# Four edits in one decoder layer: output weights split earlier, two transposition turns inside products, one FFN weight prepared ahead, the last roots on ScalarE and VectorE

## The chip, the cores and the metric

One core of one Trainium2 chip runs the program. The metric is device microseconds for one execution. PE is the matrix engine (TensorE), PEld its weight loads, DVE VectorE, ACT ScalarE, POOL GpSimd, SP the engine whose queue issues most of the transfers.

## What is computed

One layer of a decoder for a prompt group (16 meta tokens and 512 tokens) and a sample group (8 sequences of 8 new tokens with 2048 cached ones). D_MODEL is 1024, D_FF 2816. In the words of the reference:

```python
xn = rmsnorm(x, p['ln_mix_pre'])
h = xn @ p['w_in']                        # q, k, v, DeltaNet inputs and two gates
o_a = differential attention of q, k, v   # with its own rmsnorm
o_b = gated DeltaNet of the rest          # with its own rmsnorm
mix = jax.nn.sigmoid(gate_a) * (o_a @ p['w_branch_a']) + jax.nn.sigmoid(gate_b) * (o_b @ p['w_branch_b'])
x = x + rmsnorm(mix @ p['w_out'], p['ln_mix_post'])
xn = rmsnorm(x, p['ln_ffn_pre'])
up, gate = jnp.split(xn @ p['w_ffn_in'], 2, axis=-1)
gate, new_ffn_conv = causal_dwconv(gate, ffn_conv_buf, p['ffn_conv_w'], p['ffn_conv_b'])
x = x + rmsnorm((jax.nn.gelu(gate) * up) @ p['w_down'], p['ln_ffn_post'])
```

The new keys, values, states and convolution tails are outputs too. All arrays are float32.

## The kernel before

**Products.** Every float32 product is three matmuls of halves: high by high, high by low, low by high. `split` (L311 to L314) makes the halves: ScalarE copies the array rounded into `hi` (L313), VectorE subtracts that from the array into `lo` (L314). Weights come through `load_w` (L306 to L309) in blocks of 256 KB into a ring of three raw slots (`wraw`); a slot is free once cast and subtract have read it. The blocks are issued on SP's queue, each in its turn. `whi` has 2 slots and `wlo` 4. PSUM is handed out by tags (d, t, g, s); two d banks alternate.

**Order.** The program is written stage by stage; a scheduler of the framework turns it into one fixed list for each engine, and an engine that waits holds up what is behind it in its list. The last part of `main` and what follows:

- the gates, then `branch_a`, the attention branch: 8 tiles m of 128 output channels, each as two parts of 256 and 322 tokens (`branch`), a part being 12 matmuls. Behind each part a VectorE multiply-add (L1532) takes the PSUM bank into the gate's array, which frees the bank.
- `mix`: the same 8 tiles for the DeltaNet branch; then the sum of both branches (L1564) and its split for the output projection. Behind tiles 2 to 5 `load_wout` loads and splits two blocks each of the first half of w_out (`owhi`, `owlo` of `wo0`): 8 loads, 8 casts, 8 subtracts.
- `out_proj`: `product(i, g)` multiplies token tile i (0 is the sample group) by half g of w_out, 24 matmuls of 512 columns; `finish(i)` scales, adds the residual, and scales again for the FFN into `y`; `turn(i)` transposes `y` by 8 matrix-engine transposes in two groups of four, each group in a PSUM bank, and casts and splits the banks (`fhi`, `flo`). `product(4,0)` stands behind `turn(1)`. At its end come the first gate product `g0`, the first up product `u0` and `turn(4)`.
- `ffn_in`: the FFN tiles. The up weight of tile 1 is split at its start, in `plain_w` (`hw`, `lw`), and is first used right behind `turn(4)`.
- `ffn_out`: the down projection for five token tiles. The end of each is `known` and `finish`: sums of squares to a root, then the scaling of `yn` and its transfer out. The root is a power on GpSimd (`pow` with -1/2, L2175).

**Rooms.** `gt` is a ring of 18 arrays that the mixed activations use until the output projection is over; `flot2` is one of the arrays that the FFN's first stage uses later.

## Time and profile before

| what | us |
|---|---|
| median of 3 runs | 1143.41 (1142.62 to 1145.4) |
| profiled execution | 1143.95 |
| its span | 1142.2 |
| PE busy in the span | 1113.5 |
| DVE, ACT, POOL busy | 727.1, 524.7, 224.8 |

The granted matrix clock was 0.998 of full speed. The span runs from the first to the last instruction of the profiled execution; the 1.75 us between span and time lie around it. Times within the span count from its start. A timeline row reads: start, length, engine, line, operation, written array <- read arrays, size, count; in brackets how long the engine stood idle before it and who released it. One row may hold several instructions (x2), and lengths of neighbours may overlap by a tenth of a microsecond, since a next one starts before the last has written all. A matmul row's length is modelled, so the step from one start to the next is what it costs.

### The profile page before, as it was taken

The page shows a single profiled execution, that of the slowest core. Times are in us where ns is not written, and L with a number is a line of the kernel's source. Part 1 is how long each engine was busy: PE and PEld are TensorE (multiplying, and loading weights), DVE is VectorE, ACT ScalarE, POOL GpSimd, SP SyncE. Part 2 cuts the span into 40 slices and gives each one's busy share as a digit, 9 for nine tenths or more (in the row PEclk, how much of TensorE's full clock was granted, in tenths as well). Part 3 has the DMA queues.
Part 4 walks back from the last instruction along what each step waited for, and adds up shares of the span by engine and source line. Part 5 has one row for each costly group of instructions (what it writes and reads, how often), then busy time and mean ns, then how long its engine had stood idle before and what let it go on. Part 6 is the DMA issues. An engine that isn't in the chain of part 4 may idle for free.

```text
span 1142.2 us, 22715 instructions
## 1 busy us (share of the span) xinstructions
PE 1113.5 (97%) x8263; PEld 976.5 (85%) x8263; DVE 727.1 (64%) x1876; ACT 524.7 (46%) x1257; POOL 224.8 (20%) x349
## 2 busy tenths in 40 slices
PE   8999999999999999999999999999999999999997
PEld 6987897787787787789999977899999999988885
DVE  5466656695585386474343765499999999842314
ACT  5244454464465365352342444365555555732211
POOL 3122221120120020010000003334445454200000
PEclk9999999999999999999999999999999999999999
DMA  6376426837746856822232364223333232333203
GB/s 191 82 247 183 121 71 207 275 103 257 243 150 216 289 168 215 261 72 76 56 88 72 114 183 149 87 87 94 101 93 105 87 103 75 115 109 102 98 33 120
DMA packets 167610, 156.97 MB, mean 137 GB/s; under 512 B 12540, under 2 KB 123715, under 8 KB 167498
## 3 DMA queue, kind: packets, MB, share of 16 engines
q1 hardware_dynamic: 162833, 147.14, 41.7%
q0 software_dynamic: 3264, 5.16, 1.5%
q10 hardware_dynamic: 1400, 3.22, 0.9%
q8 instruction: 65, 1.06, 0.4%
q14 instruction: 48, 0.39, 0.1%
HBM read 145.60 MB, written 9.88 MB: 136 GB/s over the span
## 4 chain that ended last, share of the span: by engine, by line
PE 75%; issue 13%; DVE 5%; ACT 3%; POOL 3%; DMA 1%; POOLq 0%; DVEq 0%; SPq 0%; ACTq 0%
PE ps_d L271 27%; PE ps_t L271 19%; PE ps_g L271 15%; PE ps_s L271 6%; PE ps_t L419 6%; ACT KT L1419 1%; PE ps_m L271 1%; DVE cy L670 1%; POOL grr L383 1%; POOL gf L383 0%; DMA page<-in_cache_v 0%; POOL hss L383 0%; DVE row L990 0%; DVE row L991 0%; DVE xc L992 0%
## 5 line engine op out<-in xcount | busy, mean ns | idle before, releaser
L314 DVE TENSOR_TENSOR wlo<-wraw,whi 128x512 fp32r<-128x512 f32 x190 | 143.1, 770 | 117.8 <-ACT whi L313 117.1
L271 PE MATMUL ps_d<-xhi,whi 128*128 128x256 f32 (+2 forms) x704 | 217.2, 309 | 0.4 <-ACT xhi L313 0.3
L271 PE MATMUL ps_d<-xhi,wlo 128*128 128x256 f32 (+2 forms) x704 | 212.8, 302 | 0.5 <-POOL wlo L314 0.5
L271 PE MATMUL ps_d<-xlo,whi 128*128 128x256 f32 (+2 forms) x704 | 212.2, 302 | 0.3 <-DVE xlo L314 0.3
L313 ACT CAST whi<-wraw 128x512 fp32r<-128x512 f32 x194 | 116.3, 621 | 174.9 <-PE ps_d L271 81.1
L271 PEld LDWEIGHTS ps_d<-xhi,whi 128*128 128x128 f32 x704 | 132.9, 189 | 6.2 <-issue 3.8
L271 PEld LDWEIGHTS ps_d<-xlo,whi 128*128 128x128 f32 x704 | 133.3, 189 | 3.2 <-issue 2.4
L271 PEld LDWEIGHTS ps_d<-xhi,wlo 128*128 128x128 f32 x704 | 133.1, 189 | 2.4 <-issue 1.0
L314 DVE TENSOR_TENSOR lw<-sw,hw 128x512 fp32r<-128x512 f32 x76 | 69.2, 911 | 5.9 <-ACT hw L313 5.9
L1419 ACT COPY KT<-ps_t 128x512 f32<-128x512 f32 x106 | 57.2, 603 | 31.2 <-PE ps_t L419 30.7
L419 PE MATMUL ps_t<-consts,page 128*128 128x128 f32 x512 | 67.8, 279 | 0.3
L271 PE MATMUL ps_t<-fhit,hw 128*128 128x290 f32 x228 | 68.0, 298 | 0.0
L271 PE MATMUL ps_t<-flot,hw 128*128 128x290 f32 x228 | 67.7, 297 | 0.0
L271 PE MATMUL ps_t<-fhit,lw 128*128 128x290 f32 x228 | 67.6, 297 | 0.0
L419 PEld LDWEIGHTS ps_t<-consts,page 128*128 128x128 f32 x512 | 55.5, 140 | 13.6 <-issue 6.7
L313 ACT CAST hw<-sw 128x512 fp32r<-128x512 f32 x76 | 47.0, 618 | 32.9 <-PE ps_g L271 15.7
L271 PEld LDWEIGHTS ps_t<-flot,hw 128*128 128x128 f32 x228 | 43.2, 190 | 0.0
L271 PEld LDWEIGHTS ps_t<-fhit,lw 128*128 128x128 f32 x228 | 43.1, 189 | 0.0
L271 PEld LDWEIGHTS ps_t<-fhit,hw 128*128 128x128 f32 x228 | 43.0, 189 | 0.0
L271 PE MATMUL ps_s<-page,pT 128*32 128x256 f32 x512 | 35.3, 385 | 2.0 <-DMA page<-in_cache_v 1.8
L1912 DVE SCALAR_TENSOR_TENSOR fy<-fpre,fw,fy 128x592 f32<-128x592 f32 x44 | 36.5, 829 | 1.0 <-ACT fy L1910 0.4
L271 PE MATMUL ps_s<-KT,qb 128*32 128x256 f32 x512 | 35.7, 385 | 0.6
(688 smaller groups left out, 2847.9 us busy)
## 6 DMA issues: line engine op xcount, KB each, us to landing
page<-in_cache_k SPq DMA_DIRECT2D x128, 256.0 KB, 4.1
page<-in_cache_v SPq DMA_DIRECT2D x128, 256.0 KB, 4.5
wraw<-in_w_in SPq DMA_DIRECT2D x88, 256.0 KB, 3.0
wraw<-in_w_ffn_in SPq DMA_DIRECT2D x50, 256.0 KB, 3.0
wraw<-in_w_down SPq DMA_DIRECT2D x44, 256.0 KB, 2.6
raw<-in_w_ffn_in SPq DMA_DIRECT2D x38, 256.0 KB, 2.8
wraw<-in_w_out SPq DMA_DIRECT2D x16, 256.0 KB, 2.7
x<-in_x_prompt SPq DMA_DIRECT2D x4, 512.0 KB, 6.8
```

Of the source, the lines that this page charges most:

```text
L271: return self.nc.tensor.matmul(out, lhsT, rhs, **kw).ins
L313: self.nc.scalar.copy(hi, raw)
L314: (eng or self.nc.vector).tensor_tensor(out=lo, in0=raw, in1=hi.bitcast(F32), op=ALU.subtract)
L383: nc.gpsimd.tensor_tensor(out=dst, in0=dst, in1=self.mhalf[:rows, :n], op=ALU.pow)
L419: self.nc.tensor.transpose(out, in_, self.ident[:k, :k])
L670: nc.vector.scalar_tensor_tensor(out=y, in0=pre[:, j : j + n], scalar=self.cw[:, ch, 24 + j : 25 + j], in1=y, op0=ALU.mult, op1=ALU.add)
L1419: copy(kt[:, :, 128 * j : 128 * j + 128], tp)
L1912: nc.vector.scalar_tensor_tensor(out=y, in0=pre[:, j : j + 592], scalar=fw[:, m, 16 + j : 17 + j], in1=y, op0=ALU.mult, op1=ALU.add)
```

## The change

- **Output weights.** The arrays of w_out's first half are allotted before the attention branch. A new function `wout_ahead` issues the blocks, two after each tile m of `branch_a`, up to four times; what is left of the four would follow in `mix` from tile 2 on.
- **Turns.** `turn(0)` is issued inside `product(2,1)` and `turn(1)` inside `product(3,0)`, after k = 3 (`MID`), that is after 12 of 24 matmuls.
- **FFN weight.** The up weight of tile 1 is loaded and split at the end of `out_proj`, its high half into `flot2`, its low half into two arrays of the `gt` ring; `turn(4)` now stands amid the product that uses it.
- **Last roots.** `finish` of `ffn_out` takes Sqrt on ScalarE, then one Newton step with two reciprocals on VectorE. Sqrt needs its function table; a first Sqrt on zeros at the start of `ffn_out` brings the load there.

```diff
                         yield from self.mix_parts(self.pool(s2, "mix"))
+                        self.wo0 += self.wout_tiles(self.pool(swo, "wo0", side="right"), 0)
...
             for half in HALF_Q:
                 self.branch(m, 1, x, half)
                 yield 0.0
+            self.wout_ahead()
...
+    def wout_ahead(self):
+        if self.wo0 and self.wo_next < 4:
+            self.load_wout(self.wo0, 0, self.wo_next)
+            self.wo_next += 1
...
-            if 2 <= m < 6:
-                self.load_wout(wo0, 0, m - 2)
+            if m >= 2:
+                self.wout_ahead()
...
                 end = self.mm(p[:n], ml, whi[:, k], start=False, stop=k == 7)
+                if between and k == MID:
+                    turn(between[0], end, between[1])
...
-        product(2, 1)
+        product(2, 1, (0, "t"))
         finish(2)
-        turn(0, ends[2, 1])
-        product(3, 0)
-        turn(1, ends[3, 0])
+        product(3, 0, (1, "t"))
         product(4, 0)
...
+        hi, los = self.t(self.ftpool, [128, 8, 128], "flot2", F32R), []
+        for k, raw in zip((0, 4), self.raw_w(a["w_ffn_in"][0], 128)):
+            lo = self.t(self.gtpool, [128, 4, 128], "gt", F32R, bufs=18)
+            self.split(hi[:, k : k + 4], lo, raw)
+            los += [lo[:, j] for j in range(4)]
...
-        sts[1]["wu"] = plain_w(0, 1)
...
+        roots = [self.t(pool, [128, 5], f"yroot{j}") for j in range(3)]
+        nc.scalar.activation(roots[1], ss[:, :, 0], AF.Sqrt)
...
-            nc.gpsimd.tensor_tensor(out=r[:n], in0=r[:n], in1=self.mhalf[:n, :1], op=ALU.pow)
+            nc.scalar.activation(w, v, AF.Sqrt)
+            nc.vector.reciprocal(u, w)
+            nc.vector.scalar_tensor_tensor(out=v, in0=v, scalar=u, in1=w, op0=ALU.mult, op1=ALU.add)
+            nc.vector.reciprocal(r[:n], v)
```

How this moves instructions, at three places. Lines of the code after are larger by 2 (L314 becomes L316, L1532 becomes L1534, L271 becomes L273, L419 becomes L421).

**VectorE in the attention branch.** Before, each tile has its weight's subtract (`wlo`) and two multiply-adds into the gate's array:

```order
L314 TENSOR_TENSOR wlo_8659<-wraw_8656,whi_8658 128x512 [waits DMAHW3_49,Activation_49]
L1532 SCALAR_TENSOR_TENSOR gt_7253<-gt_7253,ps_d_8621 128x256 [waits PE_49]
L1532 SCALAR_TENSOR_TENSOR gt_7253<-gt_7253,ps_d_8641 128x322 [waits PE_49]
L314 TENSOR_TENSOR wlo_8693<-wraw_8690,whi_8692 128x512 [waits DMAHW4_49,Activation_49]
L1532 SCALAR_TENSOR_TENSOR gt_7489<-gt_7489,ps_d_8655 128x256 [waits PE_49]
```

After, from the subtract of tile 1's weight on (`wlo_8672`; `wlo_8714` is tile 2, `wlo_8756` tile 3; `gt_7253` is tile 0's array, `gt_7489` tile 1's, `gt_7617` tile 2's):

```order
L316 TENSOR_TENSOR wlo_8672<-wraw_8669,whi_8671 128x512 [waits DMAHW5_49,Activation_49]
L1534 SCALAR_TENSOR_TENSOR gt_7253<-gt_7253,ps_d_8626 128x256 [waits PE_49]
L316 TENSOR_TENSOR owlo_1604_8455<-wraw_8744,owhi_1603_8454 128x4x128 [waits DMAHW1_49,Activation_49]
L1534 SCALAR_TENSOR_TENSOR gt_7253<-gt_7253,ps_d_8646 128x322 [waits PE_49]
L316 TENSOR_TENSOR wlo_8714<-wraw_8711,whi_8713 128x512 [waits DMAHW0_49,Activation_49]
L316 TENSOR_TENSOR owlo_1604_8455<-wraw_8748,owhi_1603_8454 128x4x128 [waits DMAHW2_49,Activation_49]
L1534 SCALAR_TENSOR_TENSOR gt_7489<-gt_7489,ps_d_8668 128x256 [waits PE_49]
L1534 SCALAR_TENSOR_TENSOR gt_7489<-gt_7489,ps_d_8688 128x322 [waits PE_49]
L316 TENSOR_TENSOR wlo_8756<-wraw_8753,whi_8755 128x512 [waits DMAHW3_49,Activation_49]
L316 TENSOR_TENSOR owlo_1604_8455<-wraw_8786,owhi_1603_8454 128x4x128 [waits DMAHW4_49,Activation_49]
L1534 SCALAR_TENSOR_TENSOR gt_7617<-gt_7617,ps_d_8710 128x256 [waits PE_49]
```

The subtract of w_out's fifth block (`wraw_8744`) now stands between the two multiply-adds of tile 0, those of the sixth (`wraw_8748`) and seventh (`wraw_8786`) ahead of the first multiply-add of tiles 1 and 2. The eighth stands between tile 2's two. The same loads on SP's queue, from tile 1's weight to tile 3's:

```order
L311 DMA wraw_8669<-in_w_branch_a 128x4x128 [waits DMAHW3_49,DVE_49]
L311 DMA wraw_8702<-in_w_out 128x4x128 [waits DMAHW4_49,DVE_49]
L311 DMA wraw_8706<-in_w_out 128x4x128 [waits DMAHW2_49,DVE_49]
L311 DMA wraw_8711<-in_w_branch_a 128x4x128 [waits DMAHW6_49,DVE_49]
L311 DMA wraw_8744<-in_w_out 128x4x128 [waits DMAHW7_49,DVE_49]
L311 DMA wraw_8748<-in_w_out 128x4x128 [waits DMAHW5_49,DVE_49]
L311 DMA wraw_8753<-in_w_branch_a 128x4x128 [waits DMAHW1_49,DVE_49]
```

Two blocks of w_out stand between the weights of neighbouring tiles; before, the attention weights followed each other without a gap.

**PE around turn 1.** Before, the end of `product(3,0)` (`ps_s_9554`), the two groups of `turn(1)` (`y_9360` is tile 1's `y`), and the start of `product(4,0)`:

```order
L271 MATMUL ps_s_9554<-owhi_1668_8896,gt_9239 128x512
L419 MATMUL ps_t_9583<-consts_66,y_9360 128x128 [waits DVE_49]
L419 MATMUL ps_t_9583<-consts_66,y_9360 128x128 x3
L419 MATMUL ps_t_9588<-consts_66,y_9360 128x128 [waits DVE_49,PE_49]
L419 MATMUL ps_t_9588<-consts_66,y_9360 128x128 x3
L271 MATMUL ps_t_9597<-owhi_1668_8896,gt_8933 128x512 [waits DVE_49,PE_49]
```

After, the same turn with its neighbours, both of `product(3,0)`:

```order
L273 MATMUL ps_s_9554<-owhi_1603_8454,gt_9083 128x512
L421 MATMUL ps_t_9567<-consts_66,y_9360 128x128 [waits DVE_49]
L421 MATMUL ps_t_9567<-consts_66,y_9360 128x128 x3
L421 MATMUL ps_t_9572<-consts_66,y_9360 128x128 [waits DVE_49,PE_49]
L421 MATMUL ps_t_9572<-consts_66,y_9360 128x128 x3
L273 MATMUL ps_s_9554<-owhi_1603_8454,gt_9121 128x512
```

Twelve matmuls of `product(3,0)` now stand between turn 1 and `product(4,0)`, which still takes a t bank; turn 0 stands likewise amid `product(2,1)`.

**PE around turn 4.** Before, the end of the second gate product (`ps_g_9932`), turn 4 (`y_9622`) and the start of the second up product (`ps_s_9959`):

```order
L419 MATMUL ps_t_9874<-consts_66,y_9622 128x128 [waits DVE_49,PE_49]
L419 MATMUL ps_t_9874<-consts_66,y_9622 128x128 x3
L271 MATMUL ps_g_9932<-flo_1739_9255,fhit_1827_9840 128x290
L271 MATMUL ps_g_9932<-fhi_1738_9254,flot_1828_9841 128x290
L419 MATMUL ps_t_9879<-consts_66,y_9622 128x128 [waits DVE_49,Activation_49]
L419 MATMUL ps_t_9879<-consts_66,y_9622 128x128 x3
L271 MATMUL ps_s_9959<-fhi_1734_9250,hw_9916 128x290 [waits Activation_49]
L271 MATMUL ps_s_9959<-flo_1735_9251,hw_9916 128x290
L271 MATMUL ps_s_9959<-fhi_1734_9250,lw_9917 128x290 [waits DVE_49]
```

After, ten products of the second up product (`ps_s_9958`) stand ahead of turn 4:

```order
L273 MATMUL ps_g_9931<-fhi_1738_9254,flot_1828_9841 128x290
L273 MATMUL ps_s_9958<-fhi_1734_9250,flot_1831_9850 128x290
L273 MATMUL ps_s_9958<-flo_1735_9251,flot_1831_9850 128x290
L273 MATMUL ps_s_9958<-fhi_1734_9250,gt_9855 128x290
...
L421 MATMUL ps_t_9885<-consts_66,y_9622 128x128 [waits DVE_49,PE_49]
L421 MATMUL ps_t_9885<-consts_66,y_9622 128x128 x3
L421 MATMUL ps_t_9890<-consts_66,y_9622 128x128 [waits PE_49,Activation_49]
L421 MATMUL ps_t_9890<-consts_66,y_9622 128x128 x3
L273 MATMUL ps_s_9958<-flo_1735_9251,flot_1831_9850 128x290
```

The product's waits on ScalarE and VectorE are gone from its row in the order, and turn 4 stands later in it.

More of the change, by code (lines that the diff above doesn't have):

```diff
@@ L142 @@
 PLAIN = 3
+MID = 3
 KT = 16
@@ L248, in run @@
                     self.banks = "ggsttdd"
-                    swo = ExitStack()
-                    wo0 = self.wout_tiles(self.pool(swo, "wo0", side="right"), 0)
-                    self.mix(wo0)
+                    self.mix()
             sf = ctx.enter_context(ExitStack())
@@ L1593, in out_proj, with product @@
         ys, sums, ends = {}, {}, {}
-        def product(i, g):
+        def product(i, g, between=None):
             c0, n = self.TILES[i]
@@ L1633, in finish, with turn @@
             self.scaled(xs[:n], x[:n], r[:n], lnf[:n], CUT_O)
-        def turn(i, end):
+        def turn(i, end, tag="t"):
             n, xs, ps = self.TILES[i][1], ys.pop(i), []
@@ L1959, in plain_w @@
         def plain_w(c0, m):
-            if m == 1 and c0:
-                return w1
-            if m != 1:
-                return self.weight(w, c0 + 128 * m)
-            his, los = [], []
-            for raw in self.raw_w(w, c0 + 128 * m):
-                hi, lo = (self.t(w7, [128, 4, 128], tag, F32R, bufs=n) for tag, n in (("hw", 6), ("lw", 6)))
-                self.split(hi, lo, raw)
-                his += [hi[:, k] for k in range(4)]
-                los += [lo[:, k] for k in range(4)]
-            return his, los
+            return w1[0 if c0 else 1] if m == 1 else self.weight(w, c0 + 128 * m)
         def copy_g(st, half, ps):
```

17 lines of the change are left out of this document (10 added, 7 removed).

## The prediction

> **What bounds the kernel now.** I read the page first, then busy time by stage, then what PE waited for, then the rows of the four places that the change touches.
>
> ```profile
> span 1142.2 us, 22715 instructions
> PE 1113.5 (97%) x8263; PEld 976.5 (85%) x8263; DVE 727.1 (64%) x1876; ACT 524.7 (46%) x1257; POOL 224.8 (20%) x349
> ```
>
> PE has matrix work in 97% of the span. Whatever shortens the time here either takes work from PE or takes a wait from it; the change takes no product away, so only PE's 28.7 us without work are to be had, and only those at the places it touches. By stage (columns: span, busy PE, PEld, DVE, ACT, POOL, clock, DMA share, GB/s):
>
> ```profile
> 615.18:640.84 25.66, 25.66 (x195) 25.66 (x194) 12.34 (x23) 5.30 (x9) 0.00 (x0) 1.00 0.27 79
> 640.84:671.03 30.19, 27.74 (x200) 26.47 (x199) 25.45 (x45) 15.05 (x29) 0.00 (x0) 1.00 0.47 135
> ...
> 745.40:800.00 54.60, 54.60 (x406) 54.58 (x407) 53.14 (x88) 30.67 (x62) 19.63 (x24) 1.00 0.32 94
> ```
>
> The rows are the attention branch, the mix stage (DeltaNet branch) and the first FFN tiles. PE is full in the first and the last, 2.45 us short in the second. In the last VectorE has 1.5 us to spare in 54.6: a gain made ahead of it must survive it. The waits (engine and line waited for: total, times, longest):
>
> ```profile
> PE ps_d L271 <- ACT whi L313: 1.6, 1, 1.6
> ...
> PE ps_t L419 <- DVE flo L314: 1.2, 1, 1.2
> PE ps_s L271 <- DVE lw L314: 1.0, 1, 1.0
> PE ps_t L271 <- DVE flo L314: 0.7, 1, 0.7
> PE ps_t L271 <- ACT owhi L313: 0.6, 1, 0.6
> ...
> PE ps_s L271 <- ACT hw L313: 0.5, 1, 0.5
> ```
>
> The first and fifth are in the mix stage, the second and fourth behind turn 1, the third and sixth before the second FFN up product.
>
> **1. Output weights split in the attention branch.** What leaves the mix stage: in the attention branch one tile of 8 takes 3.205 us (25.66 / 8). The mix stage has 8 tiles of the same products and took 30.19 us; six output-projection products stood in it (1.4 us at 0.23 each, the step from 712.46 to 712.69 in part 2). 30.19 - 25.64 - 1.4 = **3.15 us** are lost there: 8 loads, casts and subtracts of w_out share the raw ring of three and VectorE (25.45 of 30.19 us busy). Without the 8 subtracts, 0.6 us each in a row, VectorE has about 20.6 us of work for 25.6, and the DeltaNet loads follow each other as the attention loads did before. I count the whole 3.15 as gained.
>
> What the attention branch gets: the same 8 loads, casts and subtracts, and each now stands in VectorE's order ahead of an operation that PE waits for. The order shows the subtract of the fifth w_out half-row block in front of the multiply-add (L1532 before, L1534 after) of tile 0's second part, and this multiply-add frees the PSUM bank for the second part of tile 1.
>
> ```profile
> 615.89 0.69 DVE L314 TENSOR_TENSOR wlo<-wraw,whi 128x512 fp32r<-128x512 f32 x1 [5.66 <-ACT whi L313]
> ...
> 618.59 0.49 DVE L1532 SCALAR_TENSOR_TENSOR gt<-gt,ps_d 128x322 f32<-128x322 f32 x1 [1.37 <-PE ps_d L271]
> ...
> 619.80 0.31 PE L271 MATMUL ps_d<-kt,whi 128*128 128x322 f32 x1
> ...
> 639.05 3.58 SPq L309 DMA_DIRECT2D wraw<-in_w_out  x2
> ...
> 641.96 0.62 ACT L313 CAST owhi<-wraw 128x512 fp32r<-128x512 f32 x1 [0.25 <-DMA wraw<-in_w_out]
> ```
>
> Of the ring's three slots the third load back must be subtracted before the next is issued. SP's order after is tile 2's weights, then w_out blocks 5 and 6; tile 2 reuses the slot of tile 1, free when the wlo of 615.89 ends at 616.58. Issues follow at 0.4 us: 616.6, 617.0, 617.4. From issue to cast took 2.9 us (639.05 to 641.96). So block 5 is cast at 619.9 to 620.5, subtracted (0.69) to 621.15, and the multiply-add (0.49) ends at 621.65; PE wanted the bank at 619.80: **1.85 us of stall** in place of a full PE. Behind the waiting subtract stand on VectorE tile 2's wlo (to 622.2), block 6 and tile 1's multiply-add. Tile 3's load goes out at 622.3, block 7 at 622.7, cast behind tile 3's at 625.75 to 626.35, subtracted to 627.0; the multiply-add behind it (0.42) ends at 627.4, and PE, 1.85 late, wants that bank at 626.65: **0.75**. Tile 4, issued at 626.5, is split by 630.7 and wanted at 630.55: **0.15**. Then VectorE is even with PE. Loss 2.75, net **-0.4 us**. The bounds: no stall (-3.15), if the loads land before their subtracts are due; and for every us that landing is later, each of the three stalls grows by one.
>
> ```profile
> wraw<-in_w_out SPq DMA_DIRECT2D x16, 256.0 KB, 2.7
> ...
> page<-in_cache_v SPq DMA_DIRECT2D x128, 256.0 KB, 4.5
> ```
>
> With 2.7 us, the median of these loads, the loss is 2.75 - 3 x 0.2 = 2.15; with 4.5 us, that of the cache pages under heavy traffic, it is 7.5, net +4.4. The branch moved 79 GB/s and gets some 80 more, so I stay near 2.9. The Trainium skill (DMA: Bandwidth & Descriptors, the section on where the fixed time goes) gives a load about 2.0 us of fixed time, nearly all completion, and bytes at 436 GB/s. Its 256 KB would take 2.6 us, 0.1 under the 2.7 of the row: an estimate by the page is a loss near 1.85 and a sum of -5.5, where I keep the rows' -4.6.
>
> **2. Turns amid products.** A turn is 8 transposes, then casts and subtracts out of two PSUM banks.
>
> ```profile
> 702.96 0.66 PE L419 MATMUL ps_t<-consts,y 66*128 66x66 f32 x8
> ...
> 709.08 0.60 PE L419 MATMUL ps_t<-consts,y 128*128 128x128 f32 x4
> 710.83 0.63 PE L419 MATMUL ps_t<-consts,y 128*128 128x128 f32 x4 [1.16 <-DVE flo L314]
> 712.15 0.47 PE L271 MATMUL ps_t<-owhi,gt 128*128 128x512 f32 x1 [0.69 <-DVE flo L314]
> 712.46 0.39 PE L271 MATMUL ps_t<-owlo,gt 128*128 128x512 f32 x1
> 712.69 0.62 PE L271 MATMUL ps_t<-owhi,gt 128*128 128x512 f32 x2
> ...
> 742.05 0.60 PE L419 MATMUL ps_t<-consts,y 128*128 128x128 f32 x4
> 742.40 0.38 PE L271 MATMUL ps_g<-flo,fhit 128*128 128x290 f32 x1
> ...
> 704.54 0.75 DVE L403 SCALAR_TENSOR_TENSOR y<-xr,r,lnf 128x512 f32<-128x512 f32 x1 [0.67 <-POOL r L383]
> ```
>
> Four transposes take 0.35 us when nothing waits (742.05 to 742.40), so turn 1 and its successor need 0.8 with the restart; they took 712.15 - 709.08 = 3.07. **Gain up to 2.25.** Turn 1 waits for the banks of turn 0, whose subtracts came 3 to 5 us after its transposes, and product (4,0) waits for one of turn 1's. After, turn 0 sits 12 products earlier (near 700.0; its input is ready at 698.8) and turn 1 at 706.2, its input ready at 705.3 (704.54 + 0.75). Each turn is followed by 12 products or 2.8 us of PE work in another bank, which hides its splits; turn 0's end at about 706.5, so turn 1's second four may wait 0.3. The splits move ahead of the chain of finish(2) by at most 0.9 us; turn 2 has 2.8 us to spare. If that cover failed, turn 2 would wait. I take **-2.25**, bounds -1.2 (half the waits stay: another bank, another split) and -2.25.
>
> **3. The second up weight.**
>
> ```profile
> 743.84 0.40 PE L271 MATMUL ps_s<-fhi,hw 128*128 128x290 f32 x1 [0.49 <-ACT hw L313]
> ...
> 743.91 2.01 DVE L314 TENSOR_TENSOR lw<-wraw,hw 128x512 fp32r<-128x512 f32 x2
> ...
> 745.37 0.40 PE L271 MATMUL ps_s<-fhi,lw 128*128 128x290 f32 x1 [1.00 <-DVE lw L314]
> ...
> 737.55 1.52 DVE L314 TENSOR_TENSOR flo<-ps_t,fhi 128x512 fp32r<-128x512 f32 x2 [1.99 <-ACT fhi L313]
> ...
> 740.57 0.75 DVE L403 SCALAR_TENSOR_TENSOR y<-xr,r,lnf 128x512 f32<-128x512 f32 x1
> ...
> 726.16 0.69 DVE L1610 TENSOR_TENSOR y<-ps_t,lnpost 128x512 f32<-128x512 f32 x1 [3.13 <-ACT ojunk L1608]
> ```
>
> PE waits 0.49 and 1.00, and restarts twice at about 0.3. After, both halves of the weight are split near 727 to 733, where VectorE idles up to 3.1 us at a time, and the casts and subtracts at 743 are gone. The same 24 products would end at 746.45 where they ended at 748.41: with turn 4's transposes in their new place, 10 products into the up product, I get **-2.1**. What is late next is turn 4's input. VectorE ends it at 741.32 now (740.57 + 0.75). Its order after puts turn 3's two subtracts (from 737.55, 1.4 in a row) ahead of the residual add of tile 4 (L411), which then runs at 738.95 to 740.0; square and sum on ScalarE (1.2), root on GpSimd (0.8) and the scaling (0.75) behind it end near 742.8, and the add-up or the copy that stands ahead of the scaling may cost 0.2 to 0.55 more: 743.0 to 743.35. PE wants it at 743.65. With 0.3 to 0.65 to spare it holds; with one more 0.69 operation it is 0.4 late. Then the full VectorE stretch: the two subtracts that left it free 1.2 us of its line, and the order moves tile 2's up weights forward, to 757.75 where PE wants them at 759.3. I count -2.1 as kept; bounds -1.2 (VectorE alone sets the pace) and -2.1.
>
> **4. The last roots.**
>
> ```profile
> 1132.62 0.15 DVE L2165 TENSOR_REDUCE ss<-yss 128x1 f32<-128x2 f32 x1
> 1132.80 0.15 DVE L2166 TENSOR_SCALAR ss<-ss 128x1 f32<-128x1 f32 x1
> 1134.20 0.16 DVE L2172 SCALAR_TENSOR_TENSOR r<-yss,ss 128x1 f32<-128x1 f32 x1 [1.25 <-ACT yjunk L2156]
> ...
> 1135.09 1.41 DVE L2180 SCALAR_TENSOR_TENSOR yn<-yn,r,x 128x512 f32<-128x512 f32 x2 [0.39 <-POOL r L2175]
> ...
> L1675 ACT ACT_TABLE_LOAD  x1: 1283/1283/1283, 679.1 to 679.1; - x1
> L1675 ACT ACTIVATE oss<-oss x1: 204/204/204, 680.4 to 680.4; 66x1 f32<-66x1 f32 x1
> ...
> 996.72 1.14 ACT L313 CAST whi<-wraw 128x512 fp32r<-128x512 f32 x2 [1.67 <-PE ps_d L271]
> ```
>
> Only the last of five roots is on the path. Before, 1134.20 to 1135.09 is 0.89. After: 0.16, a handover of about 0.1, a 204 ns activation (nearest shape), and three dependent VectorE steps 0.18 apart as at 1132.62 to 1132.80: 1.04. **+0.15**, bounds 0 and +0.4. The table load and first root take 1.28 + 0.2 us on ScalarE near 992, ahead of casts that PE's order now wants 7 products (1.6 us) later, with 1.67 us idle right behind: nothing.
>
> **The sum** for the profiled execution of 1143.95 us (span 1142.2 and 1.75 around it): -0.4 - 2.25 - 2.1 + 0.15 = -4.6, 1139.35. That execution is 0.54 above the median of 1143.41, from which it is 1138.8; I say **1139.0**.
>
> **Rivals.**
> - *The attention branch hides the splits.* VectorE works 12.34 of 25.66 us there and gets 5.5 more, which fits. If loads land in time no stall comes: -3.15 - 2.25 - 2.1 + 0.15 = -7.35, **1136.1**. Against it: slots of the ring come free one tile at a time. Chance 0.12.
> - *The next wait takes half.* Turn 4's input is late by the 0.4 above, VectorE's full stretch keeps part 3 at -1.2, one bank wait stays in part 2 (-1.2), part 1 is even: -2.25, **1141.1**, no difference that can be told. For it speaks the 53.14 of 54.60. Chance 0.31.
> - *Slower: landing in the attention branch.* Three loads now go out within 0.8 us. Each us of landing costs 3; with parts 2 to 4 at -4.2 and part 1 at -0.4, the time is 3.43 us over the old from (4.6 + 3.43) / 3 = 2.7 us more, 5.6 in all, and **1147**. No weight load shows that; the 4.5 of the pages gives about the old time. Chance 0.12, two thirds of it slower.
>
> **How the numbers follow.** Forecast 0.45, rivals 0.12, 0.31, 0.12. 0.3% of the time, 3.43 us, is about what a measurement of this kernel can tell from no change: faster means under 1139.98. Forecast 0.40 faster and 0.05 within; the first rival faster; the second 0.29 within and 0.02 faster; the third 0.04 within and 0.08 slower. Faster 0.54, within 0.38, slower 0.08. The range leaves out the third and the far ends of the others: 1136.0 to 1142.6.
>
> **What would show it.** In the profile after: mix stage at 25.6 to 27 us and no wait on whi or owhi in it; in the attention branch one PE wait on the multiply-add near 1.85 and a smaller one; no wait of 1 us behind turn 1; none before the second up product; last square to last scaling 0.1 to 0.2 longer. The prediction is wrong if the attention branch stays at 25.7 us or passes 30, or if waits of over 0.5 us turn up on turn 2, turn 4 or between 740 and 800.

## The result and the profile after

| what | before | after |
|---|---|---|
| median, us | 1144.53 (1142.62 to 1147.05, 6 runs) | 1137.25 (1136.37 to 1140.47, 6 runs) |
| profiled execution, us | 1143.95 | 1136.37 |
| its span, us | 1142.2 | 1134.6 |

The ratio is 0.9940, 95% interval 0.9922 to 0.9959: faster by 0.6%. The forecast of 1139.0 was 1.75 us too high. The kernel before stood at 1144.53 here and at 1143.41 when the forecast was made, so the gain was 7.3 us where 4.4 were forecast. The head of the page after:

```profile
span 1134.6 us, 22730 instructions
PE 1112.5 (98%) x8263; PEld 976.8 (86%) x8263; DVE 729.3 (64%) x1891; ACT 524.7 (46%) x1264; POOL 225.8 (20%) x344
```

PE's work is the same to 1 us and the span is 7.6 us shorter, so what went is waiting. Busy time by stage after (columns as in the prediction): attention branch, mix, output projection up to product (4,0), from there to the end of the second up product, the rest of the FFN, and the last token tile with the closing.

```profile
615.70:642.32 26.62, 26.02 (x195) 25.70 (x193) 14.40 (x27) 7.69 (x13) 0.00 (x0) 1.00 0.45 131
642.32:667.97 25.65, 25.65 (x195) 25.64 (x194) 20.91 (x37) 10.37 (x20) 0.00 (x0) 1.00 0.27 80
667.97:708.31 40.34, 40.34 (x187) 30.48 (x184) 20.76 (x40) 18.04 (x41) 8.35 (x10) 1.00 0.56 170
708.31:742.70 34.39, 34.38 (x215) 30.41 (x214) 18.20 (x33) 16.05 (x35) 13.30 (x19) 1.00 0.41 128
742.70:1123.78 381.08, 380.93 (x2442) 356.19 (x2441) 283.48 (x501) 182.82 (x378) 114.36 (x152) 1.00 0.31 92
1123.78:1134.60 10.82, 4.42 (x37) 4.21 (x35) 5.57 (x17) 2.04 (x8) 0.00 (x0) 0.83 0.37 138
```

The same stages before, behind the first two that the prediction shows:

```profile
671.03:712.15 41.12, 39.27 (x180) 29.52 (x178) 21.43 (x42) 20.07 (x45) 10.20 (x12) 1.00 0.57 180
712.15:748.41 36.26, 34.77 (x214) 30.53 (x215) 19.43 (x33) 14.84 (x34) 10.74 (x16) 1.00 0.30 94
748.41:1129.15 380.74, 380.74 (x2442) 356.08 (x2441) 280.64 (x490) 182.57 (x372) 112.95 (x154) 1.00 0.30 94
1129.15:1142.20 13.05, 4.45 (x37) 4.24 (x35) 4.63 (x11) 1.64 (x6) 1.10 (x2) 0.83 0.27 101
```

PE's busy time now fills the second, third and fourth stage to within a hundredth. In the first it has lost 0.6 us, and the last is 2.2 us shorter, with hardly any matrix work in it. The six output-projection products that stood in the mix before (about 1.4 us) stand in the third stage after. With that, the steps make this account (the end of a span is printed to 0.1 us, and the last row is no better than that):

| stretch | before | after | difference | forecast |
|---|---|---|---|---|
| up to the attention branch | 615.18 | 615.70 | +0.52 | 0 |
| attention branch | 25.66 | 26.62 | +0.96 | +2.75 |
| mix, without the six products | 28.81 | 25.65 | -3.16 | -3.15 |
| output projection, with them | 42.50 | 40.34 | -2.16 | -2.25 |
| (4,0) to the end of the second up product | 36.26 | 34.39 | -1.87 | -2.1 |
| FFN up to the last token tile | 380.74 | 381.08 | +0.34 | 0 |
| last token tile, to the last scaling | 5.94 | 6.10 | +0.16 | +0.15 |
| last scaling to the end | 7.11 | 4.72 | **-2.39** | 0 |

The differences add up to -7.60, the difference of the spans. They hold for these two executions. The waits of the order before change from one execution to the next: in the five profiles that have its mix stage (this one and, of the runs below, `before_again`, `roots_only`, `turns_only` and `up_only`) that stage took 30.19, 28.59, 30.37, 29.49 and 28.72 us, and the wait of 1.6 us on `whi` is in the first and the third alone. The stretch from (4,0) to the end of the second up product took 36.26, 35.65 (`roots_only`) and 35.63 us (`wout_only`) where no fall of the clock lies in it. After the change both are steady: 25.64 or 25.65 us in the mix of eight profiles, 34.35 to 34.40 in the other stretch of eight. So the mix gains 1.6 to 3.3 us and the other stretch 1.2 to 1.9, and the account shows values from the upper part of both. Behind 600 us PE has one wait left where six of 0.5 us and more are shown above:

```profile
PE ps_d L273 <- DVE gt L1534: 0.6, 1, 0.6
```

The turns and the second up product after:

```profile
704.64 1.04 PE L421 MATMUL ps_t<-consts,y 128*128 128x128 f32 x8
705.43 0.48 PE L273 MATMUL ps_s<-owhi,gt 128*128 128x512 f32 x1
...
739.61 0.29 PE L273 MATMUL ps_s<-fhi,flot 128*128 128x290 f32 x1
739.92 1.06 PE L421 MATMUL ps_t<-consts,y 128*128 128x128 f32 x8
...
739.02 0.75 DVE L405 SCALAR_TENSOR_TENSOR y<-xr,r,lnf 128x512 f32<-128x512 f32 x1 [0.44 <-POOL r L385]
```

Turn 1 now is one row of eight transposes, 0.79 us from its start to the next product (3.07 before). Turn 4 starts 0.31 us behind the product ahead of it, where one product takes 0.13: its input ends at 739.02 + 0.75 = 739.77, PE wanted it at 739.74.

The last root after, from the scaled sum to the scaling that uses it:

```profile
1128.80 0.16 DVE L2178 SCALAR_TENSOR_TENSOR yroot<-yss,ss 128x1 f32<-128x1 f32 x1 [0.73 <-ACT yjunk L2161]
...
1129.23 0.16 DVE L2182 RECIPROCAL yroot<-yroot 128x1 f32<-128x1 f32 x1
1129.43 0.22 DVE L2183 SCALAR_TENSOR_TENSOR yroot<-yroot,yroot,yroot 128x1 f32<-128x1 f32 x1
1129.69 0.16 DVE L2184 RECIPROCAL r<-yroot 128x1 f32<-128x1 f32 x1
1129.88 1.41 DVE L2189 SCALAR_TENSOR_TENSOR yn<-yn,r,x 128x512 f32<-128x512 f32 x2
```

From 1128.80 to 1129.88 are 1.08 us (forecast 1.04, 0.89 before). The 2.4 us that the end lost lie behind this row, where no working engine has anything to do. The closing instructions of the program show them. The rows of the last line of the kernel before, from the trace (times in ns: shortest, median, longest; then first and last start):

```profile
L2271 POOLq DRAIN  x3: 40/107/6880, 1134.5 to 1141.9; - x3
L2271 SPq DRAIN  x3: 7/7/7, 1138.9 to 1141.6; - x3
```

and of the kernel after:

```profile
L2280 POOLq DRAIN  x3: 40/107/7457, 986.3 to 1134.3; - x3
L2280 SPq DRAIN  x3: 7/7/7, 1133.7 to 1134.0; - x3
```

Each engine's list ends in drains. SP's first one starts when the last transfer out has landed: 1138.9 before, 1133.7 after. GpSimd's first one takes 6.88 us and starts with its last instruction, the power of the last root: 1134.5 + 6.88 = 1141.4 before, 2.5 us behind SP. After, GpSimd's last instructions lie at 986 to 987, its drain is over at 993.8, and the end is set by the transfer. That is a theory so far; the second group of runs tests it.

### The profile page after: what moved, and what is told of

The parts are those of the page before. It is cut to its first block, busy times and chain, and to the rows that moved or that the text cites. A ratio compares the mean times of both kernels' runs of the same rounds, so it can differ in the third digit from the quotient of the medians.

```text
span 1134.6 us, 22730 instructions
## 1 busy us (share of the span) xinstructions
PE 1112.5 (98%) x8263; PEld 976.8 (86%) x8263; DVE 729.3 (64%) x1891; ACT 524.7 (46%) x1264; POOL 225.8 (20%) x344
## 4 chain that ended last, share of the span: by engine, by line
PE 82%; DVE 7%; issue 3%; ACT 3%; POOL 3%; DMA 2%; SPq 0%; DVEq 0%; POOLq 0%; ACTq 0%
PE ps_d L273 32%; PE ps_t L273 20%; PE ps_g L273 16%; PE ps_s L273 7%; PE ps_t L421 6%; ACT KT L1421 1%; PE ps_m L273 1%; DVE wlo L316 1%; DVE cy L672 1%; POOL grr L385 1%; DMA wraw<-in_w_ffn_in 1%; DMA page<-in_cache_v 0%; DVE gf L1745 0%; DVE fy L1926 0%; DVE row L992 0%
## 5 line engine op out<-in xcount | busy, mean ns | idle before, releaser
L273 PE MATMUL ps_d<-xhi,whi 128*128 128x256 f32 (+2 forms) x704 | 217.3, 309 | 0.6 <-ACT xhi L315 0.5
L273 PE MATMUL ps_d<-xhi,wlo 128*128 128x256 f32 (+2 forms) x704 | 213.0, 303 | 0.5 <-POOL wlo L316 0.5
L273 PE MATMUL ps_d<-xlo,whi 128*128 128x256 f32 (+2 forms) x704 | 212.4, 302 | 0.3 <-DVE xlo L316 0.3
L316 DVE TENSOR_TENSOR wlo<-wraw,whi 128x512 fp32r<-128x512 f32 x190 | 143.5, 772 | 107.2 <-ACT whi L315 106.3
L273 PEld LDWEIGHTS ps_d<-xhi,whi 128*128 128x128 f32 x704 | 133.1, 189 | 6.2 <-issue 3.8
L273 PEld LDWEIGHTS ps_d<-xlo,whi 128*128 128x128 f32 x704 | 133.4, 190 | 3.2 <-issue 2.4
L273 PEld LDWEIGHTS ps_d<-xhi,wlo 128*128 128x128 f32 x704 | 133.2, 189 | 2.4 <-issue 1.0
L316 DVE TENSOR_TENSOR lw<-sw,hw 128x512 fp32r<-128x512 f32 x76 | 69.8, 918 | 5.2 <-ACT hw L315 5.2
L421 PE MATMUL ps_t<-consts,page 128*128 128x128 f32 x512 | 67.8, 279 | 0.5
L273 PE MATMUL ps_t<-fhit,hw 128*128 128x290 f32 x228 | 68.1, 299 | 0.1
L273 PE MATMUL ps_t<-flot,hw 128*128 128x290 f32 x228 | 67.7, 297 | 0.0
L273 PE MATMUL ps_t<-fhit,lw 128*128 128x290 f32 x228 | 67.7, 297 | 0.0
L421 PEld LDWEIGHTS ps_t<-consts,page 128*128 128x128 f32 x512 | 55.5, 140 | 14.1 <-issue 7.0
L273 PEld LDWEIGHTS ps_t<-fhit,hw 128*128 128x128 f32 x228 | 43.0, 189 | 0.4 <-DVE p L1949 0.4
L273 PEld LDWEIGHTS ps_t<-flot,hw 128*128 128x128 f32 x228 | 43.3, 190 | 0.0
L273 PEld LDWEIGHTS ps_t<-fhit,lw 128*128 128x128 f32 x228 | 43.1, 189 | 0.0
L1924 ACT ACTIVATE fy<-fpre,fw 128x592 f32<-128x592 f32 x22 | 19.5, 884 | 46.3 <-DVE fpre L1884 46.3
L273 PE MATMUL ps_s<-page,pT 128*32 128x256 f32 x512 | 35.1, 385 | 2.0 <-DMA page<-in_cache_v 1.8
```

What stands on the lines that cost most here:

```text
L273: return self.nc.tensor.matmul(out, lhsT, rhs, **kw).ins
L316: (eng or self.nc.vector).tensor_tensor(out=lo, in0=raw, in1=hi.bitcast(F32), op=ALU.subtract)
L421: self.nc.tensor.transpose(out, in_, self.ident[:k, :k])
L1924: nc.scalar.activation(y, pre[:, 0:592], AF.Identity, bias=fw[:, m, 19:20], scale=fw[:, m, 16:17])
```

## The experiments

Runs of one group share a chip and the runs of the kernel before. "Stage" below is the step between two products in the profiled execution, which is read to 0.01 us (a stretch that ends with the span, to 0.1); times are told with the ratio's interval. The ratio is not that of the two medians, and the two can differ by about 0.1%. Kernels with one part alone have other line numbers.

**Each part alone.** Four kernels are the kernel before with one part of the change. `roots_only` has the last roots:

```diff
-            nc.gpsimd.tensor_tensor(out=r[:n], in0=r[:n], in1=self.mhalf[:n, :1], op=ALU.pow)
+            nc.scalar.activation(w, v, AF.Sqrt)
+            nc.vector.reciprocal(u, w)
...
```

> The kernel before with the last roots alone on ScalarE and VectorE. Theory of the prediction: only the root's own path counts, 1.04 us in place of 0.89, so +0.15 us (0 to +0.4). Rival, read from the ends of the two profiles: GpSimd's closing drain starts with its last root and lasts 6.9 us, until 1141.4 of 1142.2, and holds the end of the program; with no GpSimd work behind 990 the end comes 0.9 us after the last transfer has landed, so -2.2 us (-1.8 to -2.6), and the stretch from the start of the last scaling of yn to the end of the span shrinks from 7.1 to about 4.7 us.

`wout_only` has the output weights ahead:

```diff
+            self.wout_ahead()
...
-            if 2 <= m < 6:
-                self.load_wout(wo0, 0, m - 2)
+            if m >= 2:
+                self.wout_ahead()
```

> The kernel before with the output weights alone split in the attention branch. Theory of the prediction: three stalls of 1.85, 0.75 and 0.15 us in the attention branch against 3.15 us gained in the mix stage, -0.4 us in all. Rival, read from the profile after: raw slots are handed on in the order in which VectorE frees them, so the fifth block is asked for when the fourth is split and not behind the attention weight; one stall of 0.6 us, attention branch 26.6 us, mix stage 25.6 us and -2.2 us in all (-1.7 to -2.7).

`turns_only` has the two turns:

```diff
-        product(2, 1)
+        product(2, 1, (0, "t"))
         finish(2)
-        turn(0, ends[2, 1])
-        product(3, 0)
-        turn(1, ends[3, 0])
+        product(3, 0, (1, "t"))
```

> The kernel before with the two turns alone moved amid products. Prediction: -2.25 us (-1.2 to -2.25), no wait of PE over 0.3 us at turns 0 and 1 or behind them. Rival: in the whole change these waits vanished only since the parts ahead of them moved other work; alone, a wait of 0.5 to 1 us stays at a turn, -1.2 us.

`up_only` has the second up weight:

```diff
+        hi, los = self.t(self.ftpool, [128, 8, 128], "flot2", F32R), []
...
+        sts[1]["wu"] = plain_w(0, 1)
```

> The kernel before with the second FFN up weight alone split ahead. Prediction: -2.1 us, and both waits on hw and lw gone. Rival: VectorE's full stretch behind it (53.1 of 54.6 us busy) takes a part back, so the first part shows no wait but the time falls by 1.2 us or less, with new waits of PE on VectorE between 745 and 800.

The kernel before stood at 1144.31 (1141.22 to 1149.38, 32 runs).

| kernel | median, us | ratio, 95% | its stage against before |
|---|---|---|---|
| roots_only | 1143.02 (12 runs) | 0.9981 [0.9967, 0.9994] | last scaling to end 4.7 for 7.1 |
| wout_only | 1144.18 (12 runs) | 0.9999 [0.9982, 1.0015] | branch 26.93 for 25.66, mix 25.64 for 28.81: -1.90 |
| turns_only | 1140.64 (9 runs) | 0.9956 [0.9941, 0.9972] | output projection 38.95 for 41.12, no wait at either turn: -2.17 |
| up_only | 1143.90 (12 runs) | 0.9993 [0.9981, 1.0006] | both waits on the weight gone; (4,0) to the end of the second up product 36.00 for 36.26, with a fall of the clock in it |

The closing drain of `roots_only` lies, as in the whole change, far ahead of the end:

```profile
L2277 POOLq DRAIN  x3: 40/107/7455, 993.8 to 1141.8; - x3
```

Of the four, the roots, which were forecast to cost 0.15, gain 2.2 us by the ratio (interval 0.7 to 3.8) and 2.4 by stage. The turns gain 5.0 us by the ratio (3.2 to 6.8) and 3.7 by the medians, more than the 2.17 of their stage. The splits ahead gain 1.90 by stage against the one profile before, 0.3 to 2.1 against all five, and by time nothing that these runs tell (from 2.1 gained to 1.7 lost). The up weight loses both its waits and gains nothing that the times tell (from 2.2 gained to 0.7 lost). One reason why time and stage part is that the waits of the order before change between executions; a second is the matter of the last section.

**The drain.** `late_pool` is the kernel after, with one power on GpSimd beside the last root, whose output nobody reads:

```diff
+            if i == 3:
+                late = self.t(self.small, [128, 1], "ss", bufs=4)
+                nc.gpsimd.tensor_tensor(out=late, in0=w, in1=self.mhalf[:n, :1], op=ALU.pow)
```

> The whole change, and one more root on GpSimd: it takes the last tile's square root to a scratch column that nothing reads, so that no engine waits for it; the output is the same. Drain theory: GpSimd's closing drain starts with that root near 3 us before the last transfer goes out, lasts 6.9 us and holds the program's end; from the start of the last scaling of yn to the end of the span 7.0 us in place of 4.7, so +2.3 us on the whole change. Path theory (the prediction): nothing waits for it, +0.0.

In the same group ran the kernel after once more, unchanged, as `after_again`, and `wout_singles` (below).

> The whole change once more, beside the other two on the same chip, as what they are read against: -7 us against the kernel before (-5 to -9), the attention branch 26.6 us, the end stretch 4.7 us.

With the kernel before at 1144.03 (12 runs), `late_pool` took 1140.10 (7 runs; ratio 0.9959 [0.9944, 0.9973]), `after_again` 1136.59 (6 runs; 0.9938 [0.9918, 0.9958]; branch 26.63 us, end 4.7, as expected). The ratios are 0.0021 apart, 2.4 us; 2.3 were expected of the drain. Their intervals overlap, so the profile has to decide. The closing of `late_pool`:

```profile
L2283 POOLq DRAIN  x3: 40/107/6900, 1131.0 to 1138.5; - x3
L2283 SPq DRAIN  x3: 7/7/7, 1135.5 to 1138.2; - x3
```

The roots are on ScalarE and VectorE, the last output has landed at 1135.5, and the end still comes at 1138.8: the drain that comes with a single small power at 1131.0 holds it for 6.9 us. From last scaling to end it takes 7.1 us, as before, against 4.7 in `after_again`. **Shown: the gain of part 4 is the closing drain of GpSimd, which follows its last instruction.**

**The branch's stalls.** Of three stalls forecast in the attention branch (1.85, 0.75 and 0.15 us) the second is there. Rows of the kernel after, by engine (SP, ScalarE, VectorE, PE):

```profile
614.21 0.37 SPq L311 DMA_DIRECT2D wraw<-in_w_branch_a  x1
615.33 2.16 SPq L311 DMA_DIRECT2D wraw<-in_w_out  x2
...
620.92 0.97 SPq L311 DMA_DIRECT2D wraw<-in_w_out  x2
...
618.54 0.62 ACT L315 CAST owhi<-wraw 128x512 fp32r<-128x512 f32 x1 [1.84 <-DMA wraw<-in_w_out]
...
624.38 0.62 ACT L315 CAST owhi<-wraw 128x512 fp32r<-128x512 f32 x1 [1.01 <-DMA wraw<-in_w_out]
...
613.48 0.69 DVE L316 TENSOR_TENSOR owlo<-wraw,owhi 128x512 fp32r<-128x512 f32 x1 [2.75 <-ACT owhi L315]
614.61 0.69 DVE L316 TENSOR_TENSOR owlo<-wraw,owhi 128x512 fp32r<-128x512 f32 x1 [0.43 <-ACT owhi L315]
616.40 0.69 DVE L316 TENSOR_TENSOR wlo<-wraw,whi 128x512 fp32r<-128x512 f32 x1 [1.10 <-ACT whi L315]
...
619.19 0.69 DVE L316 TENSOR_TENSOR owlo<-wraw,owhi 128x512 fp32r<-128x512 f32 x1 [1.47 <-ACT owhi L315]
619.80 0.48 DVE L1534 SCALAR_TENSOR_TENSOR gt<-gt,ps_d 128x322 f32<-128x322 f32 x1
...
625.03 0.69 DVE L316 TENSOR_TENSOR owlo<-wraw,owhi 128x512 fp32r<-128x512 f32 x1 [0.94 <-ACT owhi L315]
625.64 0.42 DVE L1534 SCALAR_TENSOR_TENSOR gt<-gt,ps_d 128x256 f32<-128x256 f32 x1
...
626.20 0.36 PE L273 MATMUL ps_d<-kt,whi 128*128 128x256 f32 x1 [0.60 <-DVE gt L1534]
```

Tile 2's weight (614.21) goes out before tile 1's slot is free: the subtract of tile 1's weight ends at 617.09, that of w_out's third block at 614.17 and that of the fourth at 615.30. So tile 2's weight takes the third block's slot, block 5 (615.33) the fourth's, and block 6 (617.12) tile 1's. The first four blocks are thus split ahead of the branch, which starts at 615.70, and only the other four in it: VectorE works 14.40 us there, 12.34 before. Block 5 is cast at 618.54, 3.2 us behind its issue, and the multiply-add behind its subtract ends at 620.28, as PE wants the bank at 620.31; by the steps of PE's rows that costs about 0.1 us.

The one listed stall is at tile 3, behind block 7: 0.60 us, 0.85 by the steps. The two make the 0.96 that the stage lost. Block 7 went out at 620.92 and was cast at 624.38, 3.46 us later. Had that taken the 2.9 us of the forecast, its multiply-add would have ended near 625.5 and not at 626.06, and PE wanted the bank at 625.44: an estimate from these rows, by which the slower landing is most of this stall.

Five kernels ask what this stall hangs on. `wout_singles` is the kernel after with the eight blocks issued one behind each of the eight tiles and not two behind each of four:

```diff
-        if self.wo0 and self.wo_next < 4:
-            self.load_wout(self.wo0, 0, self.wo_next)
+        if self.wo0 and self.wo_next < 8:
+            self.load_wout(self.wo0, 0, self.wo_next // 2, (4 * (self.wo_next % 2),))
...
```

> The whole change with one block of w_out behind each of the 8 tiles of the attention branch in place of two behind the first four. Ring theory: from issue through landing (2.9), cast and subtract (0.6 each) a slot is taken for about 4.2 us, three slots give 2.3 loads in a tile's 3.2 us; three loads a tile are too many, two fit: the wait of 0.6 to 1.0 us on the multiply-add goes, attention branch 25.66 in place of 26.6 us, -0.9 us on the whole change. Order theory: what costs is that a subtract stands ahead of a multiply-add at all; it still does in six tiles, so the wait stays at 0.6 us or more.

It took 1137.27 (6 runs; 0.9940 [0.9922, 0.9958]), the branch 27.62 us, 1.0 more than in the kernel after:

```profile
621.87 0.36 PE L273 MATMUL ps_d<-kt,whi 128*128 128x256 f32 x1 [0.22 <-DVE gt L1534]
630.35 0.42 PE L273 MATMUL ps_d<-kt,whi 128*128 128x322 f32 x1 [0.40 <-DVE gt L1534]
639.10 0.36 PE L273 MATMUL ps_d<-kt,whi 128*128 128x256 f32 x1 [0.30 <-DVE gt L1534]
```

Fewer loads at once give more stalls, so the crowding of the ring alone was not it; spread out, a subtract of w_out stands ahead of a multiply-add in more tiles. The rest of that thought was that VectorE's order decides. `wout_pool` and `singles_pool` take these subtracts off VectorE, in the kernel after and in `wout_singles`:

```diff
-            self.load_wout(self.wo0, 0, self.wo_next)
+            self.load_wout(self.wo0, 0, self.wo_next, self.nc.gpsimd)
...
```

> The whole change with the eight subtracts of w_out in the attention branch on GpSimd (1.28 us each, idle there) in place of VectorE (0.69). Order theory: the cost in the attention branch comes from subtracts that stand in VectorE's list ahead of the multiply-adds and wait there for a load; with none there the branch takes 25.66 us in place of 26.63, no wait of PE in it, -0.95 us on the whole change. Ring theory: a slot is held 0.6 us longer, the weights of tiles 2 to 4 come later, and PE waits on whi or wlo in place of the multiply-add, 26.6 us or more.

> The same with one block behind each of the 8 tiles. Order theory: 25.66 us in the attention branch, as in the other. Ring theory: two loads a tile at 4.8 us a slot make 2.0 loads in 3.2 us, just enough: no wait here, but one in the other.

The kernel before ran here at 1145.17 (17 runs), and once more with a profile:

> The kernel before, for a second profile on the same chip: attention branch 25.66, mix stage 30.2, from the mix stage to product (4,0) 41.1, from there to the second half's first up product 36.3, last scaling to the end 7.1 us, each within 0.3, but for stretches in which the granted clock falls.

It took 1146.31, and two of its stages missed that expectation: the mix stage took 28.59 us, and the stretch from (4,0) to the second up product 38.17, with a fall of the clock in it. `wout_pool` took 1139.55 (6 runs; 0.9943 [0.9923, 0.9963]), its branch 29.31 us; `singles_pool` 1144.12 (12 runs; 0.9991 [0.9977, 1.0005]), its branch 33.78. The order theory expected 25.66 of both, and it fell too. The ring theory was right that `wout_pool` takes over 26.6, but not on `singles_pool`, nor on the wait: PE waits for the multiply-add and not for `whi` or `wlo`. In `singles_pool` (one of PE's waits; SP, ScalarE and GpSimd rows of one block; two subtracts at once):

```profile
631.90 0.36 PE L273 MATMUL ps_d<-kt,whi 128*128 128x256 f32 x1 [0.84 <-DVE gt L1534]
...
625.94 0.37 SPq L311 DMA_DIRECT2D wraw<-in_w_out  x1
630.90 0.37 SPq L311 DMA_DIRECT2D wraw<-in_w_out  x1
...
628.89 0.62 ACT L315 CAST owhi<-wraw 128x512 fp32r<-128x512 f32 x1 [3.73 <-DMA wraw<-in_w_out]
629.41 0.61 ACT L315 CAST whi<-wraw 128x512 fp32r<-128x512 f32 x1
...
629.59 1.29 POOL L316 TENSOR_TENSOR owlo<-wraw,owhi 128x512 fp32r<-128x512 f32 x1 [3.67 <-ACT owhi L315]
...
618.54 1.27 POOL L316 TENSOR_TENSOR owlo<-wraw,owhi 128x512 fp32r<-128x512 f32 x1 [3.48 <-ACT owhi L315]
619.02 1.34 DVE L316 TENSOR_TENSOR wlo<-wraw,whi 128x512 fp32r<-128x512 f32 x1 [7.59 <-ACT whi L315]
```

A block goes out at 625.94, is cast at 628.89 and subtracted from 629.59 to 630.88, and the next goes out at 630.90: each waits for the slot of the one before, 4.96 us apart, where a tile has 3.21. The attention weight's cast stands behind the block's in ScalarE's list (629.41 behind 628.89), so each tile waits for the block. A slot is held until the slowest of cast and subtract has read it, and GpSimd's subtract takes 1.29 us for VectorE's 0.69. VectorE's own subtract is slower beside GpSimd's as well (1.34 us for 0.69, last section), so these two kernels change three things at once. Their rows show both how long the slots are held and what stands in the lists of ScalarE and VectorE behind a block that is late; the shares were not separated.

The last two kernels leave the pairs that stall out of the branch. `wout_three` splits behind tiles 0 to 2 alone, the fourth pair in the mix; `wout_two` behind tiles 0 and 1, two pairs in the mix:

```diff
-            self.wout_ahead()
+            if m < 3:
+                self.wout_ahead()
```

> The changed kernel with the split of the output weight's blocks placed only behind the attention branch's tiles 0 to 2 instead of 0 to 3, the last pair split with the other two among the mix products. If the stall of 0.60 us at tile 3 is due to the pair behind tile 2 and its successor alone, the branch takes 25.7 to 26.6 us. If the mix has room for one pair more without waits, its step stays at 25.65 us and the time is up to 0.95 us below the whole change's, about 1136 beside a kernel before at 1144.5. Rival: one pair more in the mix brings back one of the waits of before (0.4 to 0.8 us printed, about 1 us of the step), and the time is the whole change's within 0.3%.

> The changed kernel with the split of the output weight's blocks placed only behind the attention branch's tiles 0 and 1, the last two pairs split among the mix products. The branch then has no subtract of the output weight ahead of a multiply-add of tile 3: 25.66 us as in the kernel before, if the order on VectorE is what stalls. If the mix has room for two pairs more, its step stays 25.65 us, and the time is 0.95 us below the whole change's. Rival: each pair moved into the mix costs 0.5 to 1 us there, as the kernel before with all its pairs there shows (28.6 to 30.2 us with 1.39 us of filler in it), and the time is 0 to 1 us above the whole change's.

With the kernel before at 1145.58 (1142.85 to 1149.54, 11 runs), `wout_three` took **1135.62** (1134.06 to 1136.82, 6 runs; 0.9906 [0.9885, 0.9927]), `wout_two` 1138.07 (6 runs; 0.9925 [0.9903, 0.9946]). Branch and mix of `wout_three`:

```profile
616.87:642.83 25.96, 25.91 (x194) 25.70 (x193) 13.27 (x25) 6.45 (x11) 0.00 (x0) 1.00 0.39 116
642.83:668.48 25.65, 25.65 (x195) 25.64 (x193) 21.92 (x39) 11.62 (x22) 0.00 (x0) 1.00 0.35 99
```

and the only wait in those of `wout_two`:

```profile
658.49 0.38 PE L273 MATMUL ps_s<-bhi,wlo 128*128 128x256 f32 x1 [0.20 <-DVE wlo L316]
```

With the last pair gone the listed stall at tile 3 is gone (the 0.31 us left in the branch are at tile 1, behind block 5), and the mix takes that pair in for nothing: 51.61 us for both stages against 52.27 in the kernel after. With two pairs the branch is at its floor of 25.65 and the mix pays 0.47, 51.77 in all. So VectorE had room for one pair more in the mix; `wout_three` is the version with the shortest stages. Its 0.66 us over the kernel after are seen in the stages alone: the intervals of the two ratios overlap, and they are from different chips.

## Why the prediction came out as it did

1. **Part 1** was forecast at -0.4 and gave -2.20. The mix side was right (-3.15, found -3.16), but it took the waits of one execution for those of the kernel: with the other profiles before it would have been 1.6 to 3.3. On the branch side the step that failed is "tile 2 reuses the slot of tile 1, free when the wlo of 615.89 ends at 616.58": the slots come free in the order in which VectorE ends its subtracts, and w_out's third and fourth block end theirs before tile 1's weight. Tile 2's load and block 5 take those slots, block 5 goes out at 615.33 and not near 617.5 (617.0 plus the 0.52 by which the whole stage is later), and the stall of 1.85 at its multiply-add is not there, nor the 0.15 at tile 4. The second one, forecast at 0.75 for tile 3 behind block 7, is there with 0.60 listed, 0.85 by the steps. That it comes near is luck: block 7 went out 2.3 us earlier than forecast (620.92 for 622.7 + 0.52) and PE was not 1.85 late, but the block took 3.46 us from issue to cast and not 2.9. So a loss of 2.75 was 0.96. That the branch gets "the same 8 loads, casts and subtracts" was wrong too: four of the eight are split ahead of it. The fit that the prediction takes from the Trainium skill (DMA: Bandwidth & Descriptors, the section on the anatomy of one DMA) stands there for transfers that GpSimd issues; these go out on SP's queue. The rival in which the branch hides all splits also came nearer than its 0.12 says.
2. **Part 2** was right: forecast -2.25, found -2.16, no wait at either turn. Its lower bound, half the waits staying, did not come.
3. **Part 3** was right in its mechanism and 0.2 too large: -2.1, found -1.87 (1.2 to 1.9 with the other profiles before). The prediction's own two end times, 746.45 and 748.41, are 1.96 apart. The input of turn 4 was to be there 0.3 to 0.65 us ahead; it came 0.03 late, which with the handover is a gap of 0.18. The warning about VectorE's full stretch behind it holds in a small size: the rest of the FFN takes 381.08 for 380.74. It is this part's: five profiles without it take 380.61 to 380.74 there, nine with it 380.92 to 381.25 (`up_only`, with it alone, 381.00). So -1.5 to -1.6 is what stays of the part between these two executions; which instructions pay it was not traced.
4. **Part 4** was forecast at +0.15, within 0 and +0.4. The root's path was right (1.08 for 1.04). The step that failed is "Only the last of five roots is on the path": the path was followed to the last scaling and taken to go on through the output's transfer, which was never checked against what ended the span. It was GpSimd's closing drain. The term lacked -2.4, outside its bounds.

Against the forecast for the profiled execution, 1139.35, the 1136.37 lacks 2.98; to rounding that is -1.80 in part 1, -2.39 in the closing, +0.09 and +0.23 in parts 2 and 3, +0.34 in the FFN, +0.52 ahead of the branch, where the change does nothing and repeats of one kernel differ by as much (615.70 and 615.14 in two executions of the kernel after), and 0.01 in the root's path. Two errors of about 2 us, both in the direction of faster, made most of it. That the range held is luck: its lower end was that of a rival with part 1 free, and the time came near it for another reason.

## What to carry to other kernels

Follow the chain to the instruction that ends the span, the closing drains among them, before a change at the end of a program is priced: moving an engine's last instruction can be worth more than the work in it. Where loads share a ring, write down for each slot which reader ends when, in the order of the engine that frees it, and only then who waits. Splitting work ahead fills idle engine time for nothing up to the point where a late block stands in a list ahead of something that the bottleneck wants; one pair less there made the two stages 0.66 us shorter than all four. And profile the kernel before more than once: the wait that a change removes may not be there in the next execution.

## What the runs showed of the hardware

**GpSimd's closing drain** took 6.88 us, 6.90, 7.46 and 7.46 in the four kernels shown. Its record starts while GpSimd's last instructions still run. In all 14 profiles it ends 6.30 or 6.31 us after the last one's end, be that a power of 128 values (before: 1135.06, drain over at 1141.36) or an operation on 128x32 (after: 987.49, over at 993.80). Drains of the other engines took at most 2.3 us.

**The clock dips behind a thin stretch.** In `up_only`, behind turn 1, whose waits of 1.2 and 0.7 us it keeps (columns as above; the eighth number is the granted clock):

```profile
710.27:713.68 3.41, 1.67 (x9) 1.32 (x10) 2.21 (x6) 2.88 (x9) 1.14 (x2) 1.00 0.51 171
713.68:717.09 3.41, 3.41 (x10) 2.67 (x9) 1.08 (x2) 0.12 (x1) 0.00 (x0) 0.50 0.38 142
```

3.41 us with 1.67 of matrix work, half of turn 1's transposes among it, are followed by 3.41 us at half the clock: 3.41 x 0.5 = 1.7 us lost. `turns_only`, which keeps the waits on the up weight, has the same behind those (from 747.27). The kernel before has both thin stretches: its first profile shows no dip there, `before_again` one from 746.23. So the same wait brings a dip in one execution and none in another.

The clock's record in the traces shows a grid. Between its first rise and 1125 us the 14 profiles have ten dips: these three, and seven near 188 us, in a stage that the change leaves alone. Each lasts 3.41 us at 0.50 and begins a whole number of 3.413 us after the clock's first rise (`up_only`: 17.36 + 204 x 3.413 = 713.68). On this grid the stretch ahead of a dip has 1.17 to 1.78 us of matrix work. All other stretches have 1.80 or more, but two of `roots_only` with 1.70 and 1.75 that no dip follows. So, in these traces, a dip goes with a grid stretch that is about half idle, and how a wait falls on the grid changes from one execution to the next: in the first profile of the kernel before the two thinnest stretches at these places have 2.26 and 1.97.

Over 72 runs of the kernel before, time and mean granted clock go together (correlation -0.75): the median is 1145.95 us in 26 runs at 0.996 and 1143.94 in 19 at 0.998; one dip takes 3.41 x 0.5 / 1142 = 0.0015 off the mean. All eight profiles with turns and up weight both changed have no dip at either place; of the six others, three have one. That fits the turns' gain by time over that by stage, and the small gains of the parts that leave a thin stretch standing; the share of it was not measured, and the dips near 188 us, in seven of 14 profiles, add to the spread of every kernel. The Trainium skill (TensorE: Matmul & The Clock Gate, Part 1) tells of a free-running window of 3.4 us after whose idling the clock is halved. The grid, its step and the 0.50 agree. The page warns of idle gaps over about 3.4 us; here a window with 1.2 to 1.8 us of work in it was idle enough.

**VectorE beside GpSimd.** The subtract of `singles_pool` at 619.02 took 1.34 us, 0.69 when alone: it starts 0.48 behind GpSimd's (618.54 to 619.81) and ends 0.55 behind it. The Trainium skill (SBUF — State Buffer, the section on the two separate sides) says that of a VectorE operation with two inputs in SBUF and a GpSimd operation that reads SBUF, the one that starts first has a shared pair of ports for its whole instruction and the other is blocked; the row agrees. GpSimd is no free place for these splits.
